# A two-block transformer layer in float32: the tiles of the stage pools begin 192 bytes later

## The chip, the core and the metric

The kernel runs on one core of a Trainium2 chip. The metric is the device time of one execution in microseconds (us). Engines are named as the profile names them: PE is TensorE's matmuls, PEld its weight loads, DVE is VectorE, ACT ScalarE, POOL GpSimd, SP the engine that issues DMAs.

## The reference

Two blocks on one sequence of 512 positions, 1024 wide, all in float32:

```python
# block 1
h = rms_norm(x, norm_mix);  proj = h @ w_in
x = x + concat([block_attention(proj), gated_linear_attention(proj)]) @ w_out
x = x + cross_attention(rms_norm(x, norm_xattn), rms_norm(mem, norm_mem))
x = x + square(relu(rms_norm(x, norm_mlp) @ w_up)) @ w_down;  x = rms_norm(x, norm_final)
# block 2
n = rms_norm(x, norm_mix_pre)
merged = gate_a * (spatial_gating(n) @ w_branch_a) + gate_b * (dilated_attention(n) @ w_branch_b)
x = x + rms_norm(merged @ w_out_2, norm_mix_post)
x = x + rms_norm(square(relu(rms_norm(x, norm_mlp_pre) @ w_up_2)) @ w_down_2, norm_mlp_post)
```

## The kernel before

**Work.** Every large product is done in float32r with both operands split in a high and a low part: `mm3` (L289) issues three matmuls, high by high, high by low, low by high, each with its own weight load. All matmuls go through `mm` (L278, the instruction is at L287). `nc.tensor.matmul(ps, lhsT, rhs)` holds `lhsT` (128 columns) as the stationary operand and streams `rhs` as the moving one; the profile names the moving tile first, so `acc<-wt,as` moves `wt` past the stationary `as`. `tm` (L336) keeps an activation stationary and moves a weight unit, `fm` (L348) the other way round. Nearly all moving operands are 512 or 256 columns wide.

**Stages.** Four stages follow each other: `pm1` (attention of block 1, cross attention), `pf` (its MLP), `pm2` (mixing of block 2), `pf_2` (its MLP). Cooperative threads written out by hand (`Threads`, L56) give each engine its order of work; waits between engines are semaphores. Inside an MLP (`mlp`, L1007) the order alternates: `up(m)` (L1024) makes 24 matmuls of the moving `ah`/`al` with the stationary `wu` into a `tr` bank, then one of seven products per group (a Strassen-like scheme of `w_down`) makes 24 matmuls of the moving `wt` with the stationary `as` into `acc` or `aux` banks; `fold` (L1075) adds the banks up on DVE (`put`, L1069). The last quarter of `w_down` is done plainly: weights `whi`/`wlo` move past the stationary `hid`.

**Pools.** There are two kinds of buffers. Lasting ones live in the pools `cp` and `sb` through the whole program. Each stage has in addition a pool of its own, opened by `enter` (L139), which begins where `sb` ends; the next stage's pool takes the same space.

- lasting: `ident`, `ah`, `al`, and by tag `u8` (weight units `whi`, `wlo`, `wu`, `wt`, `raw`, and `ox`, `kv`, `ya`, `yb`, `va`), `k4` (4 KB tiles: `xn`, `x`, `px`, `rot`, `AT`), `st`, `sm`.
- of a stage: tag `k2` (2 KB tiles of `pm1` and `pm2`: `qx`, `pTh`, `pTl`, `qd`, `ks`, `ql`, `p`, `pT`, `qk`, `gate`, `sv`), tag `m8` (8 KB tiles of `pf` and `pf_2`: `relu`, `as`, `hid`), and `asum`.

Where they lie follows from the sizes, in bytes of a partition. `cp` begins at 1152 (scratch, constants); `ident` 512, `mhalf` 64, `ones` 512 and `junk` 2048 put `ah` at 4288, which is 192 past a multiple of 256. From there on `ah`, `al`, the 40 `sm` slots, the `k4`, `u8` (8448 each) and `st` buffers begin at 192 modulo 256 throughout, since each size is a multiple of 256 (`sm` is 40 slots of 64; `st`, the last of them, 4096 each). Behind them `wgate` (1024), `gmask` (160), `gn` (512), four `S` (512 each), `maskB` (1024) and `i4` (144) end at 174064. The stage's pool begins at the next multiple of 64, 174080, which is 0 modulo 256, and its slots of 2048, 8192 and 4096 bytes keep it there. Slices of 128 columns (512 bytes) and rows of 256 or 512 columns do not change an offset modulo 256. The one exception among the weights is `w_in_a`, whose rows have 264 columns: row k lies 32 k bytes further, modulo 256.

```python
    def k2(self, shape, dt=F32, name="k2"):
        return self.ph.tile(shape, dt, tag="k2", bufs=N_K2, name=self.name(name))

    def m8(self, shape, dt=F32, name="m8"):
        return self.ph.tile(shape, dt, tag="m8", bufs=N_M8, name=self.name(name))
```

Of the kernel before, what the change touches and what calls it, by code (L numbers as in the profile page):

```python
# [9 lines left out]
F32 = mybir.dt.float32  # L10
# [10 lines left out]
P = 128  # L21
# [9 lines left out]
N_K2 = 19  # L31
N_M8 = 6
SCRATCH = 1024
AHEAD = 1
WARM = 12

# [71 lines left out]
class Kernel:  # L108
# [30 lines left out]
    def enter(self, name):  # L139

        if self.phase is not None:
            self.phase.close()
        self.phase = ExitStack()
        if name is not None:
            self.ph = self.phase.enter_context(self.tc.tile_pool(name=name, bufs=1, reuse_waits="tile"))

    def sm(self, shape, name="sm"):
        return self.sb.tile(shape, F32, tag="sm", bufs=40, name=self.name(name))
# [87 lines left out]

    def weight(self, *key, ahead=AHEAD):

        self.weight_ahead(1 + ahead)
        got, w = self.loaded.pop(0)  # L240
        assert got == key, (got, key)
        return w
# [1376 lines left out]
```

## Time and profile before

| | |
|---|---|
| time, median of 3 runs (lowest, highest) | 1630.94 us (1626.89, 1631.4) |
| time of the profiled execution | 1628.2 us |
| its span, first to last instruction | 1626.4 us |
| mean granted TensorE clock | 0.991 |
| instructions | 21884, of these 8930 matmuls and as many weight loads |
| stages in the span, from the matmuls' tiles | `pm1` to about 475 us, `pf` to 808, `pm2` to 1285, `pf_2` to the end |

The span is 1.8 us shorter than the time of the same execution; what lies around it is before the first and after the last instruction. The duration of one matmul in the profile includes its way through the array and overlaps the next one, so the pace of a row of matmuls is read from the distance of their starts: the difference of two start times divided by the number of matmuls between them.

### The profile page before, as it was taken

How to read it: one execution, taken by the hardware profiler on the slowest of the kernel's cores; microseconds unless marked ns; L12 is line 12 of the kernel's file. 1: busy time of each engine (PE TensorE's matmuls, PEld its weight loads, DVE VectorE, ACT ScalarE, POOL GpSimd, SP SyncE). 2: the span in 40 equal slices, each digit the busy share in tenths (PEclk: the TensorE clock that was granted, in tenths of full speed). 3: DMA queues.
4: the chain of work that ended last, by engine and by line, in shares of the span. 5: the costliest groups of instructions: out<-in, count | busy, mean ns of one | idle time of the engine just before them, and what ended most of it. 6: DMA issues, size and time to landing. Idle time of an engine off the chain costs nothing.

```text
span 1626.4 us, 21884 instructions
## 1 busy us (share of the span) xinstructions
PE 1597.8 (98%) x8930; PEld 1350.1 (83%) x8930; DVE 970.7 (60%) x1194; ACT 687.6 (42%) x1052; POOL 531.8 (33%) x360
## 2 busy tenths in 40 slices
PE   9899999999999999999999999999999999999997
PEld 8777878898898888887799899888888988888876
DVE  4456475554566868686644554464245577686844
ACT  6456465333343535344523333374324445343431
POOL 1112220000016556573250531330021274746621
PEclk9999999999999999999999999999999999999999
DMA  8612133422242423214313302322424513232221
GB/s 286 188 41 91 47 112 109 139 77 78 76 146 78 143 78 126 82 65 156 120 50 130 104 13 93 104 78 85 162 79 155 197 63 129 91 116 82 87 91 65
DMA packets 50293, 171.08 MB, mean 105 GB/s; under 512 B 6192, under 2 KB 6720, under 8 KB 50192
## 3 DMA queue, kind: packets, MB, share of 16 engines
q1 hardware_dynamic: 50192, 169.68, 31.1%
q8 instruction: 70, 1.15, 0.3%
q14 instruction: 31, 0.25, 0.0%
HBM read 163.35 MB, written 8.93 MB: 106 GB/s over the span
## 4 chain that ended last, share of the span: by engine, by line
PE 44%; DVE 2%; POOL 2%; issue 1%; ACT 1%; DMA 0%; POOLq 0%; DVEq 0%; ACTq 0%
PE acc L287 34%; PE tr L287 7%; PE aux L287 2%; POOL raw L272 1%; PE tr L296 1%; DVE acc L1073 0%; DMA st<-in_w_down 0%; DVE as L300 0%; DVE acc L1495 0%; ACT junk L1483 0%; DVE wlo L232 0%; DVE wt L300 0%; POOL relu L1064 0%; DVE wu L232 0%; POOL fr L1491 0%
## 5 line engine op out<-in xcount | busy, mean ns | idle before, releaser
L287 PE MATMUL tr<-ah,wu 128*128 128x512 f32 x896 | 283.9, 390 | 0.0
L232 DVE TENSOR_TENSOR wlo<-st,whi 128x1024 fp32r<-128x1024 f32 (+1 forms) x158 | 200.3, 1293 | 126.3 <-ACT whi L231 102.3
L231 ACT ACTIVATE whi<-st 128x1024 fp32r<-128x1024 f32 (+1 forms) x158 | 160.6, 1044 | 206.4 <-PE acc L287 115.9
L287 PE MATMUL acc<-wt,as 128*128 128x512 f32 x864 | 210.3, 399 | 5.4 <-DVE acc L1073 3.5
L287 PE MATMUL acc<-ah,whi 128*128 128x512 f32 (+1 forms) x576 | 213.0, 372 | 0.7 <-ACT ah L299 0.7
L287 PE MATMUL acc<-al,whi 128*128 128x512 f32 (+1 forms) x576 | 212.2, 369 | 0.6 <-DVE al L300 0.6
L287 PE MATMUL acc<-ah,wlo 128*128 128x512 f32 (+1 forms) x576 | 211.7, 368 | 0.0
L300 DVE TENSOR_TENSOR wt<-raw,wt 128x1024 fp32r<-128x1024 f32 x84 | 169.2, 2028 | 59.5 <-ACT wt L299 59.5
L287 PEld LDWEIGHTS acc<-wt,as 128*128 128x128 f32 x864 | 163.9, 190 | 45.3 <-DVE acc L1073 3.9
L287 PEld LDWEIGHTS tr<-ah,wu 128*128 128x128 f32 x896 | 168.4, 188 | 35.9
L287 PE MATMUL tr<-al,wu 128*128 128x512 f32 x448 | 174.7, 390 | 0.0
L1022 POOL TENSOR_TENSOR relu<-relu 128x512 f32<-128x512 f32 x64 | 94.8, 1482 | 215.2 <-ACT relu L1021 184.8
L272 POOL TENSOR_TENSOR raw<-raw,raw 128x1024 f32<-128x1024 f32 x48 | 153.9, 3222 | 14.5 <-DMA raw<-in_w_down 9.5
L287 PE MATMUL acc<-whi,ah 128*128 128x512 f32 (+2 forms) x432 | 147.2, 349 | 2.7 <-ACT whi L231 2.7
L287 PE MATMUL acc<-wlo,ah 128*128 128x512 f32 (+2 forms) x432 | 148.3, 345 | 0.0
L287 PE MATMUL acc<-whi,al 128*128 128x512 f32 (+2 forms) x432 | 148.1, 346 | 0.0
L299 ACT ACTIVATE wt<-raw 128x1024 fp32r<-128x1024 f32 x84 | 87.9, 1055 | 90.4 <-POOL raw L272 56.6
L287 PEld LDWEIGHTS acc<-ah,whi 128*128 128x128 f32 x576 | 108.7, 189 | 19.8 <-issue 1.7
L287 PEld LDWEIGHTS acc<-ah,wlo 128*128 128x128 f32 x576 | 109.0, 189 | 18.7 <-issue 0.9
L232 DVE TENSOR_TENSOR wu<-st,wu 128x1024 fp32r<-128x1024 f32 x64 | 107.9, 1692 | 27.1 <-ACT wu L231 27.1
L287 PEld LDWEIGHTS acc<-al,whi 128*128 128x128 f32 x576 | 109.2, 190 | 17.6 <-DVE al L300 0.8
L287 PEld LDWEIGHTS tr<-al,wu 128*128 128x128 f32 x448 | 84.2, 188 | 18.1
(344 smaller groups left out, 2817.9 us busy)
## 6 DMA issues: line engine op xcount, KB each, us to landing
st<-in_w_up SPq DMA_DIRECT2D x64, 512.0 KB, 3.8
raw<-in_w_down SPq DMA_DIRECT2D x48, 512.0 KB, 4.7
st<-in_w_in_2f SPq DMA_DIRECT2D x44, 512.0 KB, 4.4
st<-in_w_in_u SPq DMA_DIRECT2D x20, 512.0 KB, 4.9
st<-in_w_out SPq DMA_DIRECT2D x16, 512.0 KB, 4.7
st<-in_w_down SPq DMA_DIRECT2D x16, 512.0 KB, 4.2
st<-in_w_xk SPq DMA_DIRECT2D x8, 512.0 KB, 5.0
st<-in_w_xv SPq DMA_DIRECT2D x8, 512.0 KB, 4.5
```

Of the source, the lines that this page charges most:

```text
L231: nc.scalar.activation(hi[:, s, :], st, AF.Copy)
L232: nc.vector.tensor_sub(lo[:, s, :], st, f32(hi[:, s, :]))
L272: nc.gpsimd.tensor_sub(r[name][:, s, :], r[x][:, s, :], r[y][:, s, :])
L287: self.nc.tensor.matmul(ps, lhsT, rhs, start=start, stop=stop, skip_group_check=more)
L296: self.nc.tensor.transpose(ps, src, self.ident)
L299: self.nc.scalar.activation(hi, src, AF.Copy)
L300: self.nc.vector.tensor_sub(lo, src, f32(hi))
L1022: nc.gpsimd.tensor_mul(t, t, t)
```

## The change

`enter` takes one more tile from each stage's pool, before any other: 48 float32 numbers in each partition, 192 bytes. Nothing writes or reads it. The tiles of the pool that are taken after it begin 192 bytes later: 174272 instead of 174080, that is 192 instead of 0 modulo 256, as `ah`, `al` and the `u8` and `k4` buffers do. The last byte of the largest pool moves from 227328 to 227520. All four stage pools move alike, so that which tile of a stage lies over which tile of the stage before stays as it was. No instruction is added, removed or moved in the program.

```diff
--- before.py
+++ after.py
@@ -31,6 +31,8 @@
 N_K2 = 19
 N_M8 = 6
 SCRATCH = 1024
+
+PAD = 48
 AHEAD = 1
 WARM = 12
 
@@ -143,6 +145,7 @@
         self.phase = ExitStack()
         if name is not None:
             self.ph = self.phase.enter_context(self.tc.tile_pool(name=name, bufs=1, reuse_waits="tile"))
+            self.ph.tile([P, PAD], F32, tag="pad", bufs=1, name=self.name("pad"))
 
     def sm(self, shape, name="sm"):
         return self.sb.tile(shape, F32, tag="sm", bufs=40, name=self.name(name))
```

## Rows read from the trace of the kernel before

**Rows 1.** The page's first part: busy us (share of the span) and instructions by engine.

```profile
PE 1597.8 (98%) x8930; PEld 1350.1 (83%) x8930; DVE 970.7 (60%) x1194; ACT 687.6 (42%) x1052; POOL 531.8 (33%) x360
```

**Rows 2.** Groups by line and shape: count, busy us, mean ns, idle before and releasers.

```profile
L287 PE MATMUL acc<-wt,as 128*128 128x512 f32 x864 | 210.3, 399 | 5.4 <-DVE acc L1073 3.5 <-DVE x L1073 2.0
...
L287 PE MATMUL acc<-whi,hid 128*128 128x512 f32 x256 | 81.1, 396 | 0.0
...
L287 PE MATMUL acc<-wlo,hid 128*128 128x512 f32 x128 | 50.6, 395 | 0.0
...
L287 PE MATMUL acc<-ah,wu 128*128 128x256 f32 x256 | 47.2, 284 | 0.2 <-ACT ah L299 0.2
...
L287 PE MATMUL aux<-wt,as 128*128 128x512 f32 x144 | 34.6, 395 | 0.0
...
L287 PE MATMUL aux<-kv,qx 128*128 128x256 f32 x96 | 12.7, 282 | 0.0
```

**Rows 3.** Chain that ended last, second MLP: start us, us, what, number of instructions.

```profile
1317.87 5.60 PE acc L287 x24
1323.47 5.47 PE tr L287 x24
...
1389.87 10.91 PE tr L287 x48
```

**Rows 4.** Timeline of PE, 424 to 432 us and 1608 to 1612 us.

```profile
424.32 0.62 PE L287 MATMUL acc<-whi,ox 128*128 128x512 f32 x2
...
427.05 0.40 PE L287 MATMUL aux<-pTh,kv 128*128 128x512 f32 x1
...
428.44 0.63 PE L287 MATMUL acc<-whi,ox 128*128 128x512 f32 x2
...
1608.19 0.63 PE L287 MATMUL acc<-whi,hid 128*128 128x512 f32 x2
...
1611.69 0.63 PE L287 MATMUL acc<-whi,hid 128*128 128x512 f32 x2
```

**Rows 5.** Timeline of PE: 264-wide moving `w_in_a`, then `ah` stationary with step 4.

```profile
17.64 0.29 PE L287 MATMUL acc<-wlo,ah 128*128 128x264 f32 x1
...
22.03 0.28 PE L287 MATMUL acc<-wlo,ah 128*128 128x264 f32 x1
...
857.83 0.40 PE L287 MATMUL acc<-wlo,ah 128*128 128x512 f32 x1
...
861.83 0.39 PE L287 MATMUL acc<-whi,ah 128*128 128x512 f32 x1
```

**Rows 6.** Chain that ended last, towards the end of the second MLP.

```profile
1483.68 4.21 PE acc L287 x18
1487.90 10.08 POOL raw L272 x3
...
1555.68 0.61 DVE acc L1073
...
1556.33 5.49 PE acc L287 x12
```

**Rows 7.** Busy us of each engine by stretch, then granted clock, DMA share, GB/s.

```profile
475.00:800.00 325.00, 323.00 (x1456) 265.44 (x1455) 226.02 (x163) 132.99 (x157) 173.88 (x86) 1.00 0.31 104
...
1285.00:1572.00 287.00, 283.55 (x1266) 233.10 (x1265) 203.36 (x131) 123.26 (x147) 168.72 (x73) 0.99 0.29 99
...
744.00:748.00 4.00, 2.00 (x9) 1.35 (x8) 4.00 (x7) 0.70 (x3) 0.95 (x1) 1.00 0.57 190
...
1556.00:1560.00 4.00, 3.67 (x9) 2.90 (x10) 3.73 (x4) 1.54 (x2) 3.65 (x2) 0.50 0.44 160
```

**Rows 8.** DMA issues: number, KB each, median us from issue to landing.

```profile
st<-in_w_up SPq DMA_DIRECT2D x64, 512.0 KB, 3.8
...
gain<-in_ln_v_gain SPq DMA_DIRECT2D x1, 256.0 KB, 4.5
```

## The prediction

> **What bounds the kernel now.** I read the page's busy times first: PE is busy in 98% of the span, DVE in 60%, ACT in 42%, POOL in 33% [rows 1]. With 8930 matmuls back to back, nothing but the pace of the matmuls, their number and the few holes in PE can move the time. The number stays, so the question is whether an address can change the pace.
>
> For that I took the chain that ended last in a quiet part of the second MLP, where it runs through PE alone. It shows the `tr` blocks of `up` and the product blocks side by side: 24 matmuls with `as` stationary take 5.60 us, 233.3 ns each; 24 with `wu` stationary take 5.47 us, 227.9 ns; and 48 of the latter in a row take 10.91 us, so the second 24 take 5.44, 226.7 ns [rows 3]. Width, type, count of weight loads and moving layout are the same; both stand in the same stretch, beside the same work of the other engines. What differs is where the stationary operand lies: `wu` at 192 modulo 256 like its moving `ah`, `as` at 0 while its moving `wt` is at 192.
>
> Then the timeline, to see whether the pool tile is to blame or the product. `tm` with the stationary `ox` (lasting, 192) starts 12 matmuls in 2.73 us, 227.5 ns; `tm` with the stationary `hid` (stage pool, 0), the same function with the same tile shape, starts 15 in 3.50 us, 233.3 ns; and with the roles turned, `pTh`/`pTl` (stage pool) moving past the lasting `kv`, six take 1.39 us, 231.7 ns [rows 4]. So wherever a 512-wide matmul takes one operand from each kind of buffer, it is 4 to 6.6 ns slower than where both are lasting.
>
> That the way in which the stationary operand is read can matter at all is seen in the value products of block 2, where `ah` is taken with a step of four: 17 matmuls in 4.00 us, 235 ns, though both operands are lasting [rows 5].
>
> **The change part by part.** The pad is never accessed: no instruction, no wait, and the overlaps from stage to stage are kept. Its whole effect is that the mixed pairs (0 against 192) become equal pairs (192 and 192), as those of 226.7 ns are. The count of the pairs:
>
> - `as` stationary: 864 + 144 = 1008 [rows 2], now at 233.3. The new pace lies between 226.7 (a block that goes on without settling) and 227.9 (a block that first has to settle as the `tr` block behind an `as` block does) [rows 3]: 5.4 to 6.6 ns each, 5.4 to 6.7 us. I take the middle, 6.1 us.
> - `hid` stationary: 256 + 128 = 384 [rows 2], 233.3 to 226.7 or 227.5 [rows 3, 4]: 2.2 to 2.5 us, taken 2.3.
> - `pTh`/`pTl` moving: four heads of 12, 48 in all, 231.7 to 227.5 [rows 4]: 0.2 us.
> - The `tr` blocks behind `as` blocks: 1008 / 24 = 42 of them, and each loses 5.47 - 5.44 = 0.03 us on settling [rows 3]. If equal pairs before them leave nothing to settle, that is 1.3 us; if the block change itself is the cause, nothing. Taken 0.6.
> - `qx` stationary under the 256-wide `kv`: 96, mean 282 ns against 284 for the lasting pair of that width [rows 2]. Here the mixed pair is the quicker one: a loss of 96 x 2 ns = 0.2 us.
> - Other engines' accesses to the shifted tiles: no row before shows an operation at the new offset of its own tile, so the nearest are DVE's and POOL's shares in the MLPs, 226 and 174 of 325 us, 203 and 169 of 287 [rows 7]. With 30% of DVE free, a few per cent either way stay hidden; nothing taken.
> - Six transfers go to stage tiles, such as `gain` for the layer norm: 256 KB in 4.5 us at offset 0, while 512 KB to `st` at 192 land in 3.8 us [rows 8]. No gain of offset 0 is seen; they are not on the chain; nothing taken.
>
> **What is given back.** Not all of the gain reaches the end. Towards the end of the second MLP the chain leaves PE: from 1487.90 us it goes through POOL, ACT, DVE and a weight transfer, and comes back to PE at 1556.33, when a DVE `fold` lets it go on [rows 6]; PE waits 3.5 us there [rows 2]. What PE saves in these 68.4 us it only waits longer: at 5.60 + 5.47 us for a pair of blocks [rows 3], 6.2 blocks of 24 matmuls at 6.1 ns, 0.9 us lost. The first MLP has the same code and the wait `x L1073` of 2.0 us [rows 2]; I take the same 0.9.
>
> The sum: 6.1 + 2.3 + 0.2 + 0.6 - 0.2 - 1.8 = 7.2 us, against the profiled execution's 1628.2: 1621.0. That execution is 2.7 us under the median of the three timed runs and 1.3 over their lowest; the four together average 1629.4, so I put the time at 1622.
>
> Bounds: upward in gain 6.7 + 2.5 + 0.2 + 1.3 - 0.2 with nothing given back, 10.5 us, 1617.7 against the same execution. Downward: 5.4 + 2.2 + 0.2 + 0 - 0.2 - 1.8 = 5.8, and less if the longer waits cost clock. After the 3.5 us wait the granted clock was 0.50, 1.2 GHz, and 12 matmuls took 5.49 us, against 2.80 at the full clock (half of 5.60); after the 2.0 us wait of the first MLP it stayed at 1.00 [rows 2, 3, 6, 7]. If a wait of 2.9 us there drops it as well, 2.7 us go: a gain of 3.1, 1625.1.
>
> **Rivals.**
>
> *The low address bits don't matter; the stage pool's place does, or something else that the pad leaves as it is.* All pairs of 231 ns and more but the step-4 case reach above byte 174080, and all of 227 stay below it, so offset and place cannot be told apart by them. For this rival: the 264-wide weights, whose rows pass through all eight multiples of 32 modulo 256 under a stationary at 192, start 36 matmuls in 4.39 us, 122 ns each with no slow rows among them [rows 5]; and the 256-wide mixed pair is no slower [rows 2]. Against it: the place would have to matter for moving and stationary alike, and the step-4 case is slow far below 174080. The time: as before, 1628 to 1631. By the Trainium skill (TensorE: Matmul & The Clock Gate, Step-by-step: what each phase is for) matmul and weight load have independent read ports and loading the next tile doesn't steal bandwidth from the running matmul, by which offsets could do nothing and this rival would hold. The trace gives that rule no full support: equal work runs at 226.7 and at 233.3 ns.
>
> *The gain is swallowed.* The waits behind DVE take more than 1.8 us and the clock falls in the first MLP too: 1624 to 1627.
>
> *The separation helped.* Today stage tiles at 0 and PE's lasting operands at 192 lie apart; once all are at 192, ACT, DVE and POOL may get in the way of PE's reads, and the 226.7 ns of the lasting pairs become 233.3. Every 100 matmuls cost 0.66 us; it decides against the change once some 1,100 of the lasting ones (7.2 / 0.0066) turn slow, and is slower by 0.3% beyond 1,840. If the `tr` blocks (1,344) and as many others slowed, 17.7 us less the 7.2, 1641. Against it: DVE, ACT and POOL use lasting tiles at 192 all the time already, and the `tr` blocks beside them run at 226.7 [rows 3, 7].
>
> **Chances.** Forecast 0.62 (1617.5 to 1625), swallowed 0.08 (1624 to 1627), no effect 0.24 (1627 to 1632), separation 0.06 (1636 and more). 0.3% of 1630.94 is 4.9 us, about what a measurement of this kernel can tell from no change: faster means under 1626.0, slower over 1635.8. Faster: nearly all of the first and half of the second, 0.65. Slower 0.06, same 0.29. The range leaves out the last case, the upper third of the no-effect case and a little below: 1616 to 1630. The likeliest case's own range is 1617.5 to 1625.
>
> **What would show it.** Right: in the new profile product blocks of 24 take 5.44 to 5.47 us instead of 5.60, `hid` rows 227 ns, `pTh` 227, the 256-wide `kv` under `qx` a shade slower, and PE's waits on `fold` a little longer than 3.5 and 2.0 us. Wrong: blocks still at 5.60 (the place, not the offset), `tr` blocks above 5.47 (separation), or blocks at 5.44 with a later return to PE at the ends of the MLPs (swallowed).

## The result and the profile after

| | before | changed |
|---|---|---|
| median of 4 runs (lowest, highest) | 1629.57 us (1626.89, 1631.4) | 1621.49 us (1621.05, 1623.04) |
| profiled execution, its span | 1628.2, 1626.4 us | 1621.62, 1619.8 us |

The ratio is 0.9949, with a 95% interval of 0.993 to 0.9968: 8.1 us faster by the medians, 6.6 by the profiled executions. 1622.0 had been forecast. The number of instructions is the same, 21884; lines from 146 on are three further on in the profile (L290 is what L287 was).

The page's first part, beside [rows 1]: PE is 9.0 us less busy, the others are where they were.

```profile
PE 1588.8 (98%) x8930; PEld 1350.9 (83%) x8930; DVE 971.9 (60%) x1194; ACT 686.3 (42%) x1052; POOL 530.8 (33%) x360
```

The groups by shape, beside [rows 2]. The product blocks' group is 4 us shorter, although more of its matmuls than before run at half clock (below), and the idle time before it has grown from 5.4 to 7.1; the 256-wide `kv` under `qx` has gone from 282 to 284 ns, level with `wu`.

```profile
L290 PE MATMUL acc<-wt,as 128*128 128x512 f32 x864 | 206.3, 395 | 7.1 <-DVE acc L1076 3.7 <-DVE x L1076 3.4
...
L290 PE MATMUL acc<-whi,hid 128*128 128x512 f32 x256 | 79.5, 390 | 0.0
...
L290 PE MATMUL aux<-kv,qx 128*128 128x256 f32 x96 | 13.0, 284 | 0.0
```

The chain that ended last in the second MLP (start us, us, what, number), beside [rows 3, 6]: the product blocks and the `tr` blocks now take the same 5.44 us, 226.7 ns a matmul, and two `tr` blocks in a row take just twice that, so nothing has to settle any more.

```profile
1316.70 5.44 PE acc L290 x24
1322.14 5.44 PE tr L290 x24
...
1387.42 10.88 PE tr L290 x48
...
1484.09 10.06 POOL raw L275 x3
...
1551.64 4.60 PE acc L290 x12
```

The timeline of PE, beside [rows 4]: six matmuls of `pTh`/`pTl` start within 1.36 us (226.7 ns, 231.7 before), 18 of `hid` within 4.08 (226.7 ns, 233.3 before). The two rows between them are the first MLP's wait: a product block stops half way for the fold, 3.38 us.

```profile
426.95 0.39 PE L290 MATMUL aux<-pTh,kv 128*128 128x512 f32 x1
...
428.31 0.62 PE L290 MATMUL acc<-whi,ox 128*128 128x512 f32 x2
...
738.07 2.88 PE L290 MATMUL acc<-wt,as 128*128 128x512 f32 x12
744.33 5.49 PE L290 MATMUL acc<-wt,as 128*128 128x512 f32 x12 [3.38 <-DVE x L1076]
...
1600.08 0.62 PE L290 MATMUL acc<-whi,hid 128*128 128x512 f32 x2
...
1604.16 0.62 PE L290 MATMUL acc<-whi,hid 128*128 128x512 f32 x2
```

The same wait before:

```profile
742.07 2.96 PE L287 MATMUL acc<-wt,as 128*128 128x512 f32 x12
747.02 3.06 PE L287 MATMUL acc<-wt,as 128*128 128x512 f32 x12 [2.00 <-DVE x L1073]
```

And the granted clock behind that wait, by stretch (busy us of PE, PEld, DVE, ACT, POOL, then clock, DMA share, GB/s): before, it was 1.00 at this place [rows 7]; now the 12 matmuls that follow run at half clock, 1.2 GHz, 427 ns from start to start, and take 5.49 us instead of 3.06.

```profile
739.00:743.00 4.00, 1.95 (x9) 1.30 (x7) 4.00 (x6) 2.91 (x5) 0.00 (x0) 1.00 0.10 33
743.00:747.00 4.00, 2.67 (x6) 2.15 (x7) 3.82 (x6) 1.54 (x2) 2.64 (x1) 0.53 0.68 234
```

**Where the time came from, and where some of it went.** The two traces have the same matmuls in the same order, so the start of one and the same matmul can be compared:

| matmul | before, us | after, us | difference |
|---|---|---|---|
| first of `pf`, 256-wide `wu` | 475.10 | 474.84 | -0.26 |
| fourth of the product block that waits in the first MLP | 742.77 | 738.75 | -4.02 |
| first behind that wait | 747.02 | 744.33 | -2.69 |
| 11th of the `tr` block behind it | 752.22 | 752.10 | -0.12 |
| in the transposes that end `pf` | 806.56 | 805.21 | -1.34 |
| first of `pf_2` | 1285.36 | 1284.20 | -1.16 |
| first of the product block that waits in the second MLP | 1549.92 | 1545.02 | -4.90 |
| first behind that wait | 1556.33 | 1551.64 | -4.69 |
| second of the `tr` block behind it | 1562.04 | 1556.32 | -5.72 |
| near the end of the `hid` rows | 1617.06 | 1610.05 | -7.01 |

Each MLP gains 3.7 us in its product part and 1.2 to 1.3 from there to its end, where the `hid` rows are. In the first, 1.3 us go to the longer wait and 2.6 to the clock behind it. In the second the wait takes 0.2, and the clock, which fell there before as well, costs 1.0 less than it did. The mixing stages gain and lose nothing to speak of. These are two executions, one of each kernel; which of the clock's terms belong to the change is taken up behind the experiments.

### The profile page after: what moved, and what is told of

Same layout as the page of the kernel before. It is cut to its first block, busy times and chain, and to the rows that moved or that the text cites. A ratio compares the mean times of both kernels' runs of the same rounds, so it can differ in the third digit from the quotient of the medians.

```text
span 1619.8 us, 21884 instructions
## 1 busy us (share of the span) xinstructions
PE 1588.8 (98%) x8930; PEld 1350.9 (83%) x8930; DVE 971.9 (60%) x1194; ACT 686.3 (42%) x1052; POOL 530.8 (33%) x360
## 4 chain that ended last, share of the span: by engine, by line
PE 44%; POOL 2%; DVE 2%; issue 1%; ACT 1%; DMA 0%; POOLq 0%; DVEq 0%; ACTq 0%
PE acc L290 34%; PE tr L290 7%; PE aux L290 2%; POOL raw L275 1%; PE tr L299 1%; DVE acc L1076 0%; DVE as L303 0%; DVE acc L1498 0%; DMA st<-in_w_down 0%; ACT junk L1486 0%; DVE wlo L235 0%; DVE wt L303 0%; POOL relu L1067 0%; DVE wu L235 0%; POOL relu L1025 0%
## 5 line engine op out<-in xcount | busy, mean ns | idle before, releaser
L290 PE MATMUL tr<-ah,wu 128*128 128x512 f32 x896 | 283.2, 389 | 0.0
L290 PE MATMUL acc<-ah,whi 128*128 128x512 f32 (+1 forms) x576 | 213.2, 372 | 0.8 <-ACT ah L302 0.8
L290 PE MATMUL acc<-wt,as 128*128 128x512 f32 x864 | 206.3, 395 | 7.1 <-DVE acc L1076 3.7
L290 PE MATMUL acc<-al,whi 128*128 128x512 f32 (+1 forms) x576 | 212.1, 369 | 0.6 <-DVE al L303 0.6
L290 PE MATMUL acc<-ah,wlo 128*128 128x512 f32 (+1 forms) x576 | 211.7, 368 | 0.0
L290 PEld LDWEIGHTS acc<-wt,as 128*128 128x128 f32 x864 | 164.8, 191 | 42.5 <-DVE acc L1076 4.2
L290 PEld LDWEIGHTS tr<-ah,wu 128*128 128x128 f32 x896 | 168.4, 188 | 34.9
L290 PE MATMUL tr<-al,wu 128*128 128x512 f32 x448 | 174.3, 389 | 0.0
L290 PE MATMUL acc<-whi,ah 128*128 128x512 f32 (+2 forms) x432 | 146.7, 347 | 1.2 <-ACT whi L234 1.2
L290 PE MATMUL acc<-wlo,ah 128*128 128x512 f32 (+2 forms) x432 | 147.6, 344 | 0.3 <-DVE wlo L235 0.3
L290 PE MATMUL acc<-whi,al 128*128 128x512 f32 (+2 forms) x432 | 147.4, 344 | 0.0
L290 PEld LDWEIGHTS acc<-ah,whi 128*128 128x128 f32 x576 | 108.7, 189 | 19.8 <-issue 1.7
L290 PEld LDWEIGHTS acc<-ah,wlo 128*128 128x128 f32 x576 | 109.0, 189 | 18.7 <-DVE wlo L235 0.9
L290 PEld LDWEIGHTS acc<-al,whi 128*128 128x128 f32 x576 | 109.2, 190 | 17.5 <-DVE al L303 0.8
L290 PEld LDWEIGHTS tr<-al,wu 128*128 128x128 f32 x448 | 84.3, 188 | 17.4
```

What stands on the lines that cost most here:

```text
L290: self.nc.tensor.matmul(ps, lhsT, rhs, start=start, stop=stop, skip_group_check=more)
```

## The experiments

In each, the time of the kernel before was taken on the same chip between the runs; ratios are to that. By its medians, from 1628.5 to 1629.57 us, the kernel before itself differs by 1.1 us from round to round, so that medians of two other kernels are compared no more closely than that. A pace is given as the length of a block of 24 matmuls in the chain.

**A pad of 256 bytes: the place without the offset.**

```diff
-PAD = 48
+PAD = 64
```

> The pad is 256 bytes instead of 192: the pools move and have the pad, but the stage tiles stay at 0 modulo 256. Theory A (the low address bits of the two operands have to agree): nothing is gained; product blocks of 24 take 5.60 us, hid rows 233 ns, the time is that of the kernel before, 1629 within 2 us. Rival B (the pad or the later place itself gives the gain): blocks of 5.44 us and a time of 1621.5.

1628.73 against 1628.74 us, ratio 1.0004 (0.9987 to 1.002). The chain of its second MLP:

```profile
1322.18 5.60 PE acc L290 x24
1327.78 5.47 PE tr L290 x24
```

To the hundredth the blocks of [rows 3]. Neither the pad nor the later place does anything; rival B falls.

**A pad of 64 bytes: equal modulo 64 and 128, not modulo 256.**

```diff
-PAD = 48
+PAD = 16
```

> Stage tiles at 64 modulo 256, the lasting ones at 192: equal modulo 128, not modulo 256. Theory A with a period of 256: blocks stay near 5.60 us, time 1629. Theory A with a period of 128: blocks of 5.44 us, time 1621.5. Rival C (only the offset of the stationary operand by itself counts, 0 being the bad one): 5.44 too, so C and the shorter period are left to the next kernels.

1629.29 against 1628.74, ratio 1.0007 (0.9994 to 1.002).

```profile
1319.43 5.59 PE acc L290 x24
1325.02 5.46 PE tr L290 x24
```

No gain: agreement modulo 128 isn't enough, and it isn't offset 0 by itself that is bad, for here the stage tiles lie at 64.

**A pad of 128 bytes.**

```diff
-PAD = 48
+PAD = 32
```

> Stage tiles at 128 modulo 256, the lasting ones at 192: unequal modulo 128 and modulo 256. Theory A with either period: blocks near 5.60 us, time 1629. Rival C (offset 0 alone is bad): 5.44 us and 1621.5.

1625.52 against 1628.74, ratio 0.9985 (0.9975 to 0.9995).

```profile
1318.22 5.49 PE acc L290 x24
1323.72 5.44 PE tr L290 x24
```

Between the two expectations. 5.49 us, 228.8 ns, so a third of the excess is left, and the `tr` blocks behind it need no settling. It matters how the two offsets lie to each other, and not only whether they are equal.

**All buffers at 0.** A gap of 64 bytes ahead of everything; with the pad of 192 the stage tiles are at 0 too.

```diff
+        cp.tile([P, 16], F32, name="front")
         self.ident = cp.tile([P, P], F32, name="ident")
```

> A gap of 64 bytes ahead of all lasting buffers puts ah, al, k4 and u8 at 0 modulo 256, and with the pad of 192 the stage tiles lie at 0 too: all pairs equal, at another offset than in the changed kernel. Theory A: as in the changed kernel, blocks of 5.44 us, 1621.5 within 2 us. Rival C (a stationary operand at 0 is read more slowly): 5.60 us for every block, tr blocks included, some 4,800 matmuls 6.6 ns longer, 32 us more: 1653.

1622.02 against 1628.74, ratio 0.9964 (0.9952 to 0.9976).

```profile
1316.13 5.44 PE acc L290 x24
1321.57 5.44 PE tr L290 x24
```

The same blocks as in the changed kernel, at an offset that had been the "bad" one. It is the relation of the two operands and not the offset of either; rival C falls.

**The other way round: `ah` and `al` apart from the rest.**

```diff
         self.al = cp.tile([P, KT, T], F32R, name="al")
+        cp.tile([P, 16], F32, name="gap")
```

> The other way round: a gap of 64 bytes between al and the buffers behind it leaves ah and al at 192 modulo 256 and puts k4, u8 and the stage tiles at 0. Now the pairs of as, hid and ox with their weights are equal, and those of ah and al with every weight unit are not: 2688 matmuls of 512 columns have their stationary operand 64 past the moving one, 528 have it 192 past. Theory A: tr blocks of 24 take 5.60 us and product blocks 5.44; by the pace of the kernel before (233.2 against 226.7 ns) and of the kernel with the pad of 128 (228.9) that is 17.5 + 1.2 us, less 1296 matmuls of 256 columns that become 3.4 ns shorter (116.3 against 119.7), 4.4 us, and less up to 2 us that the waits at the ends of the MLPs take in: 1632 to 1636. Rival B (the stage pool's place): tr blocks stay at 5.44 us, 1621.5.

1633.49 against 1628.5 us, ratio 1.003 (1.0013 to 1.0048).

```profile
1330.52 5.46 PE acc L290 x24
1335.98 5.60 PE tr L290 x24
```

The two kinds of blocks have changed places: the `tr` blocks, both operands far below the stage pools, now run at 233.3 ns, and the `as` blocks have the short pace with their tiles at 0. This is the strongest single run for the forecast's reason: the effect was made at will where it had not been. Single times from 1629 to 1640 scatter more than for the other kernels.

**Filling the wait.** In both MLPs, 12 matmuls (`FILL`) whose result nobody reads, ahead of the half block that waits.

```diff
                     fold(i, c, g)
+                    if g == 2 and i == 6 and c == 0:
+                        ps = self.tr()
+                        for _ in range(FILL):
+                            self.mm(ps, self.ah[:, 0, self.cs(0)], self.ah[:, 0, :], True, True, 0.0)
                     yield
```

> The changed kernel with 12 more matmuls (ah past itself into a tr bank that is free; nobody reads the result) in each MLP, put before the matmul that waits for the last fold: 2.7 us of work inside a wait of 3.4 to 3.8 us. Theory D (a part of the gain went into the TensorE clock, which falls to 0.5 after these longer waits): the clock stays at 1.00 through both places, the matmuls after the wait run at 227 instead of 427 ns, and 4 to 5 us come back: 1617. Rival E (the clock's fall is hidden, since the chain behind the wait runs through DVE and DMA): the clock stays up and the time is unchanged, 1621.5, or up by what the 12 matmuls stick out of the wait.

1618.54 us, ratio to the kernel before 0.9947 (0.9927 to 0.9966). The median is 3.0 us under the changed kernel's, but the ratios, 0.9947 and 0.9949, don't tell the two kernels apart; what the filling does is read from the traces. The timeline of PE at the first MLP's wait, and the stretch behind it with its clock (columns as above):

```profile
738.14 2.88 PE L291 MATMUL acc<-wt,as 128*128 128x512 f32 x12
740.86 2.88 PE L291 MATMUL tr<-ah 128*128 128x512 f32 x12
744.11 3.06 PE L291 MATMUL acc<-wt,as 128*128 128x512 f32 x12 [0.37 <-DVE x L1077]
```

```profile
744.00:748.00 4.00, 3.89 (x17) 3.19 (x18) 3.80 (x5) 1.54 (x2) 3.86 (x2) 1.00 0.58 199
```

The half block behind the first wait starts at the same time as without the filling, within 0.3 us, but takes 3.06 us instead of 5.49: the clock stays at 1.00. It stays up behind the second wait too. By the starts of the same matmuls as in the table above, the wait and what follows it win 2.9 us in the first MLP, 2.6 of them by the clock, and 1.6 in the second: 4.5 us, as theory D had it. But 1.5 go again at the start of `pm2`, where the clock falls in this trace and did not in the changed kernel's (columns as above):

```profile
808.00:812.00 4.00, 4.00 (x23) 4.00 (x23) 3.73 (x5) 3.75 (x6) 2.68 (x5) 0.57 0.99 332
```

That the filling brings this about is not shown: the clock fell there too in the traces of the pad of 128 and of `ah` and `al` apart, which have none. At the last matmul 2.9 us are left.

**The same filling in the kernel before**, without the pad.

> The kernel before, without the pad, with the 12 filling matmuls in each MLP. In it only the second wait is long enough for the clock to fall (427 ns matmuls behind it), the first is not. Theory D: 2.4 us are won, 1626, and the step from here to the changed kernel with the same filling (1618.5) is the whole effect of the offsets with no clock lost to it, 7 to 8 us. Rival E: 1628.5.

1626.29 against 1629.35 us, ratio 0.9982 (0.9971 to 0.9994). From here to the filled changed kernel it is 7.75 us by the medians: about the step from before to after without filling, 8.1. So by the medians the filling is worth about 3 us to both; clear of the scatter it is here, by the interval of the ratio 1.0 to 4.7 us. The mean granted clock of the ten executions was 0.9915, that of the fifteen of the kernel before in the same rounds 0.9887. The expectation had only the second MLP's clock to win back, 2.4, holding the first wait too short for the clock to fall. That was so in the one trace it was read from, but not in others with the same paces: with the pad of 256 the clock fell behind 2.17 us, with the pad of 64 behind 2.27, and 1.5 us were lost there. With the pad of 256 (timeline of PE, then the stretch with its clock):

```profile
749.81 4.61 PE L290 MATMUL acc<-wt,as 128*128 128x512 f32 x12 [2.17 <-DVE x L1076]
```

```profile
750.00:754.00 4.00, 4.00 (x11) 3.16 (x11) 3.83 (x4) 1.54 (x2) 4.00 (x2) 0.57 0.63 203
```

**Unequal pairs for the 256-wide products.** The weight units that are used 256 columns wide begin 64 bytes (`SHIFT` = 16 float32 numbers) later within their own `u8` slot, which has 256 bytes to spare (the first four `wu` units of each MLP likewise).

```diff
+        narrow = w == 256 and (key in NARROW or (key, idx) in NARROW)
...
+        elif narrow:
+            hi, lo = (self.u8([P, SHIFT + nk * w], F32R, n)[:, SHIFT:].rearrange("p (a b) -> p a b", a=nk) for n in ("whi", "wlo"))
```

> The changed kernel with the weight units of all 256-wide products moved 64 bytes on within their u8 slots, so that 1728 matmuls of 256 columns get an unequal pair (offset 64 or 192) while all of 512 columns keep an equal one. Theory A with the sign that the 256-wide kv and qx showed (116.3 ns unequal, 119.7 equal): 3.4 ns less for each that follows its predecessor closely, some 1,500, 5 us, less some tenths for the first 512-wide matmuls behind each such block: 1617 to 1619. Rival F (an unequal pair costs at every width, and kv and qx were quicker for a reason of their own): 1621.5 or more.

1617.14 us (1612.83 to 1622.02), ratio 0.9932 (0.9913 to 0.9951), 4.4 under the changed kernel's median; the intervals of the two ratios overlap, so the time alone does not settle it. The traces do, as far as one execution of each can: the `tr` blocks behind the 256-wide head of the second MLP start 4.5 us earlier than in the changed kernel, and end 5 earlier. Of the 4.5, 2.3 were won before the first matmul of `pf`, and there traces scatter as much without any such reason (that of the pad of 256 is 2.6 us later than that of the kernel before, at the same paces). The rest is 0.6 in the first part of each MLP and 1.5 in the mixing of block 2; in the trace of the kernel with both edits, below, the MLPs' 0.6 come again. The group of the first `up` units (columns as in [rows 2]), in the changed kernel and in this one:

```profile
L290 PE MATMUL acc<-ah,wu 128*128 128x256 f32 x256 | 47.2, 284 | 0.2 <-ACT ah L302 0.2
```

```profile
L299 PE MATMUL acc<-ah,wu 128*128 128x256 f32 x256 | 45.0, 278 | 0.3 <-ACT ah L311 0.3
```

At 256 columns the sign is turned: start to start in close order, 115.0 ns with the stationary operand 64 bytes past the moving one, 117.5 with 192, 119.6 with none. Rival F falls. But the offset alone does not set this pace. The 115.0 is a mean of stretches at 113 and others at 118, and for the group above it is 113.9 here and 116.4 in the kernel with `ah` and `al` apart, where the two operands have the same offsets; what decides between them no run shows. And 128 bytes win nothing: with the pad of 64, the `kv` matmuls under `qx` are no quicker than with equal offsets (284, above):

```profile
L290 PE MATMUL aux<-kv,qx 128*128 128x256 f32 x96 | 13.0, 285 | 0.0
```

**A pad of 160 bytes**, a single execution.

```diff
-PAD = 48
+PAD = 40
```

> A pad of 160 bytes: stage tiles at 160 modulo 256, 32 below the lasting ones. If the cost falls with the distance as from 64 (233.2 ns with the stationary operand 64 past the moving one) over 128 (232.7) and 192 (228.9) to 0 (226.7), 224 gives 227 to 228 ns for product blocks, 5.45 to 5.47 us. If only full equality modulo 64 or 256 gives the short pace, 229 ns or more.

```profile
1318.23 5.59 PE acc L290 x24
1323.82 5.45 PE tr L290 x24
```

The execution took 1626.53 us, within the 1625.37 to 1634.46 of the kernel before. The block takes 5.59 us where 5.45 to 5.47 had been expected, if the cost fell with the distance: wrong. 32 bytes off cost as much as 64 or 128. By the stationary operand's distance past the moving one, modulo 256, a block of 24 takes 5.44 us (0), 5.60 (64), 5.59 (128), 5.49 (192), 5.59 (224).

**The pad in the MLPs alone.**

```diff
-            self.ph.tile([P, PAD], F32, tag="pad", bufs=1, name=self.name("pad"))
+            if name.startswith("pf"):
+                self.ph.tile([P, PAD], F32, tag="pad", bufs=1, name=self.name("pad"))
```

> The pad in the pools of the two MLPs alone; the stage tiles of the attention and mixing stages stay at 0 modulo 256. Theory A: as and hid have equal pairs, pTh, pTl and qx keep unequal ones, whose gain (48 of 4 to 5 ns) and loss (96 of 2 to 3 ns) cancel: the time of the changed kernel, 1621.5 within 1.5 us, PE in the MLPs as there. Rival G (the other two stages brought a part of the gain by something else than these pairs): 1623 or more.

1622.19 against 1629.35 us, ratio 0.9956 (0.9942 to 0.997). By the time the gain is there, but the interval reaches up to 1624.5 us, which leaves room for rival G. The trace narrows it: against the changed kernel's, the stretch before `pf` differs by 0.3 us and that of `pm2` by 0.2, while the MLPs' product parts and `hid` rows win the same as there. So rival G, which needs 1.5 us, is not borne out. In this trace the wait of the first MLP is longer than in the changed kernel's, and still the clock stays up behind it (timeline of PE, then the stretch with its clock):

```profile
744.72 3.06 PE L291 MATMUL acc<-wt,as 128*128 128x512 f32 x12 [3.50 <-DVE x L1077]
```

```profile
745.00:749.00 4.00, 4.00 (x19) 3.23 (x19) 3.81 (x4) 1.55 (x2) 4.00 (x2) 1.00 0.62 219
```

**Filling and unequal narrow pairs together.**

> The changed kernel with the filling matmuls and the moved units of the 256-wide products together: the two gains lie in different places (filling 3.0 us at the ends of the MLPs, units 4.4 us at the heads of the stages and in the attention), so they add up to 7.4 us less: 1614. If the units' gain is partly taken by a wait that only the filling had hidden, 1616.

1616.93 us (1614.04 to 1619.19), ratio 0.992 (0.9907 to 0.9932): faster than the kernel before. Its median is 4.6 us under the changed kernel's, and the two intervals meet only between 0.993 and 0.9932, so a gain over the changed kernel is likely and not quite shown; it is not the 1614 expected. Against the kernel with the moved units alone (0.9932) no difference is shown. The profiled execution was the longest of its five, 1619.19; in it the clock was lower at the start of the program, for which neither edit has a reason, 0.92 against 0.97 in the changed kernel's trace for the same stretch (this kernel's row first):

```profile
150.00:200.00 50.00, 50.00 (x313) 39.52 (x314) 21.91 (x56) 23.57 (x52) 9.80 (x10) 0.92 0.07 22
```

```profile
150.00:200.00 50.00, 50.00 (x357) 39.43 (x356) 24.30 (x59) 24.15 (x52) 9.80 (x10) 0.97 0.07 22
```

The same stretch is as low, 0.93 and 0.92, in the traces of the pad of 256 and of `ah` and `al` apart. At the first matmul of `pf` this execution is 2.4 us behind the changed kernel's, and at the start of `pm2` the clock falls as with the filling alone. How much of the missing 3 us that explains in the other four executions stays open.

## Why the prediction was right, by its steps

- **The reason.** Equal offsets give the short pace. Shown from both sides: by the four pads, by the layout at 0, and by making the short pairs long. The rival that only the place counts is refuted by the pad of 256 bytes. That the other engines' accesses slow PE, and not the pair, is not borne out either: in the kernel before the `hid` rows kept their 233 ns from 1600 to 1604 us, with DVE busy for 1.8 of the 4 us and the DMA for 1%, and from 1604 to 1608, with 3.2 us and 60%. By the Trainium skill (TensorE: Matmul & The Clock Gate, Step-by-step: what each phase is for), PE reads the moving operand and the weight load through two independent ports, and a weight load takes no read bandwidth from the running matmul. The runs show that the two operands are not without effect on each other, for the pace goes by how their offsets lie, 226.7 or 233.3 ns; whether it is the two reads that meet, no run shows.
- **`as`, taken 6.1 us.** The blocks settle at once, 5.44: 1008 x 6.6 = 6.7 us, the upper bound.
- **`hid`, 2.3.** 384 x 6.6 = 2.5 us. **`pTh`/`pTl`, 0.2:** 48 x 5.0 = 0.2. **`qx`, -0.2:** 282 to 284 ns, as forecast.
- **Settling of the `tr` blocks, 0.6.** All of it came, 42 x 0.03 = 1.3 us.
- **Other engines, nothing.** DVE 971.9 and POOL 530.8 us against 970.7 and 531.8 [rows 1]: nothing.
- **Given back, 1.8.** The waits took 1.33 and 0.22 us, 1.6 together, where 0.9 and 0.9 had been taken. With all buffers at 0 they took 1.66 and 0.31, with the pad in the MLPs alone 1.45 and 0.80 (table below). So this term was right in sum, though not in its halves.
- **The clock**, which the prediction had put into its lower bound alone, on the reading that a longer wait drops it. In the changed kernel's trace it fell behind the first wait, 2.6 us, and the second MLP lost 1.0 less than before: 1.5 us more given back. That the change brings this about is not shown, and the other traces speak against it: with all buffers at 0 and with the pad in the MLPs alone, which have the same pairs in the MLPs, the clock stayed up behind longer first waits, and with the pad of 256, at the paces and waits of the kernel before, it fell. Over all traces without filling it fell behind the first wait in seven of ten, after waits of 2.17 to 3.64 us, and stayed up in three, after 2.00, 3.50 and 3.71; behind the second it fell in all ten. In the three with filling it fell behind neither.

Time in each stretch less that of the kernel before, us, between the starts of the same matmuls as in the first table:

| stretch | changed | pad of 256 | all at 0 | pad in the MLPs alone |
|---|---|---|---|---|
| first MLP, to the block that waits | -3.76 | 0.00 | -3.76 | -3.76 |
| its wait | 1.33 | 0.18 | 1.66 | 1.45 |
| behind the wait, where the clock can fall | 2.57 | 1.54 | -0.08 | -0.03 |
| from there to the end of `pf` | -1.23 | 0.00 | -1.23 | -1.23 |
| second MLP, to the block that waits | -3.74 | -0.01 | -3.73 | -3.74 |
| its wait | 0.22 | -0.43 | 0.31 | 0.80 |
| behind the wait | -1.04 | 0.00 | 0.00 | -0.22 |

The first wait in the kernel with all buffers at 0, and the clock there (timeline of PE, then the stretch):

```profile
746.39 3.01 PE L290 MATMUL acc<-wt,as 128*128 128x512 f32 x12 [3.71 <-DVE x L1077]
```

```profile
746.00:750.00 4.00, 3.61 (x16) 3.00 (x17) 3.86 (x4) 1.54 (x2) 3.58 (x2) 1.00 0.66 192
```

- **The sum.** 6.7 + 2.5 + 0.2 + 1.3 - 0.2 - 1.6 = 8.9 us without the clock, and 7.4 with the 1.5 that it took in these two executions, against 7.0 at the last matmuls compared, 8.1 by the medians, and 7.2 forecast. The mechanism was right; that the time was hit so closely is in part luck, for two terms came out at their upper bounds, 1.3 us more than taken, and the clock took as much in the trace.
- **The separation** of stage and lasting tiles in the other engines' eyes cost nothing: the `tr` blocks went from 5.47 to 5.44, not up.

## What to carry to other kernels

Two operands that PE reads at the same time should be laid out with a known distance of their addresses, and pools that begin wherever the last odd-sized tile ends leave it to chance: read the pace of blocks of like matmuls from the distance of their starts, sort it by pool, and if it splits, one pad is the test. Measure before choosing: in this kernel 512 columns want equality modulo 256, and 256 columns were quicker 64 or 192 bytes apart, but not 128. And where the gain runs into a wait of the same engine, look at the clock behind it, in more than one execution; here a dozen matmuls that nobody needs, in each of the two holes, were worth about 3 us by the medians.

## What the runs showed that had not been expected

- Of the distances tried at 512 columns, none but 0 modulo 256 gives the short pace: 32 below costs the whole 6 ns, 64 below a third of it. Why the excess follows the distance as it does, and why it turns its sign between 256 and 512 columns, no run here shows.
- A block with equal pairs does not run at its short pace at once if it follows a block at 64 past: in the kernel before, the first six matmuls of a `tr` block behind an `as` block took 228 to 236 ns (medians over 42 blocks) before they came to 227; behind an equal one, and behind one at 192 past (the pad of 128), they started at 227.
- An equal pair takes 226.7 ns at 512 columns and 119.6 at 256, at the same granted clock. By an estimate from these two, the columns alone are 214 ns of the 226.7 (twice the difference of 107.1); the other 12.5 were not won back in any layout tried at 512 columns.
- The TensorE clock's fall does not go by the length of the wait alone: behind 2.17 us it fell with the pad of 256, behind 3.50 and 3.71 us at the same place in two other kernels it didn't. What else decides is not shown.
